# Up projection of a gated MLP: eight half-size block products per feature block become seven, with the operands of tokens and down weights made once

## The chip, the cores and the metric

The kernel runs on one core of one Trainium2 chip. The metric is the device time of one execution in microseconds; the median of three runs counts. The profiled execution is one more run, and its time is given beside its span.

## What is computed

One layer of a streaming encoder over 1024 tokens of width 1024, all in float32: a conditioned normalisation, a combined input projection that feeds four retention heads and a short convolution group, an output projection with a gated residual, and then the part that this change is about, a gated MLP with a causal width-3 convolution over time:

```python
h = modulate(rms_norm(x, norm2_g), sh2, sc2)
u = causal_dwconv(h @ w_up, conv_ffn_w, conv_ffn_b)
ua, ub = jnp.split(u, 2, axis=-1)
x = x + gt2[:, None, :] * ((jax.nn.silu(ua) * ub) @ w_down)
return rms_norm(x, final_g)
```

`w_up` is 1024 x 5632 (the a half and the b half of 2816 columns each), `w_down` is 2816 x 1024, `gt2` is one gate per output column.

## The kernel before

TensorE multiplies a float32 pair as three products of split operands: every operand x is held as hi (x rounded to the fp32r format by a ScalarE cast) and lo (x - hi, a VectorE subtraction), and `mm3` (line 115) issues hi*hi, hi*lo and lo*hi. A matmul takes a stationary 128 x 128 block and 512 moving columns.

The stages follow one another on TensorE, whose instructions keep the order of the program, as `pin` and `mm` say (lines 106 to 113):

1. Front: the first two adaLN vectors from `w_ada`, the transposed normalised tokens, and the v projection. The order of this stage is planned ahead from a table of costs (`run_steps`, line 211). `w_ada` pieces arrive as 512-byte runs (line 277).
2. The k and q projections, retention and the g projection (lines 616 to 786). Between them the other adaLN vectors are summed on VectorE from pieces of `w_ada` (`ada_step`, line 552).
3. Conv stage (line 820): twelve column pieces of `w_in`, 48 matmuls each, with two `ada_step` calls behind each piece.
4. Output projection in three groups of token blocks, (0,1,2), (3,4,5) and (6,7) (`out_mm`, line 879). `norm2` (line 897) makes the residual x1, which stays in SBUF, and its normalised form; `norm2_T` (line 910) transposes a block of 128 tokens, applies scale and shift, and splits the result into the hi and lo of `h2`, the moving operand of the up projection. `h2` is two slabs, one for each half of the tokens.
5. Up stage: for each of 22 feature blocks f, `up` (line 986) loads a 1024 x 128 piece of the a half and one of the b half (512-byte runs, line 729), splits both, and multiplies each with all tokens: 2 pieces x 2 token halves x 8 row blocks x 3 = 96 matmuls. `conv3` (line 815) applies the convolution straight from PSUM, silu and a product follow. After each two feature blocks, `acts_side` and `weights_side` make the operands of the down projection and store them to HBM; GpSimd multiplies the down weights by `gt2` there (line 1029).
6. Down stage: activations and down weights are taken as 2 x 2 blocks, and seven block products of 11 x 12 matmuls (Winograd's form of Strassen's scheme) do the work of eight. `operands` (line 1072) loads one 512 KB tile per step into a ring, casts and subtracts; results are added to x1 from PSUM.
7. Tail (line 1139 on): the last product's results are added, normalised and written.

Instructions on VectorE, ScalarE and the DMA queue of SyncE that are not pinned are ordered when the program is built, by when they are expected to be ready. Tiles come from pools: a tag with `bufs=3` has three buffers, and a tile waits for the release of the one three before it. The raw weight pieces share three buffers (tag `wr`, line 88), their hi and lo forms four each (tags `wh` and `wl`, lines 97 and 98). All DMAs are issued by SyncE.

Of the kernel before, what the change touches and what calls it, by code (L numbers as in the profile page):

```python
# [18 lines left out]
P = 128  # L19
# [51 lines left out]
def layer(ctx: ExitStack, tc: tile.TileContext, a: dict, out: bass.AP):  # L71
# [70 lines left out]
    psum = ctx.enter_context(tc.tile_pool(name="psum", bufs=1, space=PSUM))  # L142
# [24 lines left out]
    stage = slab.tile([P, 4, KT, 256], F32, tag="S2", name="stage")  # L167
# [8 lines left out]
    ada_src = a["w_ada"][:, 0:2048].rearrange("(k p) (s c) -> p k s c", p=P, s=2)  # L176

    def w_in_raw(c0, kp, name):
        raw = raw_tile(name)
        src = a["w_in"][kp * 256 : (kp + 1) * 256, c0 : c0 + 512]  # L180
        nc.sync.dma_start(raw.rearrange("p (k c) b -> p k (c b)", k=2), src.rearrange("(k p) c -> p k c", p=P))
        return raw
# [92 lines left out]
    def ada_src_dma(k, j):  # L275
        w = stage[:, k % 4]
        nc.sync.dma_start(w[:, :, j * P : (j + 1) * P], ada_src[:, :, j, k * P : (k + 1) * P])

    def ada_first(k):
        w = stage[:, k % 4]  # L280
        q_(nc.vector.tensor_scalar(out=w[:, 0], in0=w[:, 0], scalar1=scol[:, 0:1], scalar2=None, op0=ALU.mult))

    def ada_next(k, kt):
        w = stage[:, k % 4]
        q_(mul_add(w[:, 0], w[:, kt], scol[:, kt : kt + 1], w[:, 0]))

    def ada_act(k, kt):
        w = stage[:, k % 4]
        q_(nc.scalar.activation(w[:, kt], w[:, kt], AF.Copy, scale=scol[:, kt : kt + 1]))

    def ada_add(k, i, j):
        w = stage[:, k % 4]
        q_(nc.gpsimd.tensor_tensor(out=w[:, i], in0=w[:, i], in1=w[:, j], op=ALU.add))
# [3 lines left out]
    def ada_mm(k, j, e):  # L297
# [202 lines left out]
    def ada_load(dst, k0, kn, c0, cn):  # L500
        src = a["w_ada"][k0 * P : (k0 + kn) * P, c0 : c0 + cn]
# [29 lines left out]
    def ada_finish(what, hf, c, acc):  # L531
        ps = r1k(f"pada_{what}_{hf}")
        if what[0] == "g":
            dst = (gt1 if what == "g1" else gt2)[:, hf * 512 : (hf + 1) * 512]
            mm(ps, ones, acc)
            nc.vector.tensor_tensor(out=dst, in0=ps, in1=dst, op=ALU.add)
        else:
# [9 lines left out]

    ada = ada_group()
# [21 lines left out]
    cos = cst.tile([P, TB, 64], F32, name="cos")  # L570
    sin = cst.tile([P, TB, 64], F32, name="sin")
# [155 lines left out]
    def w_col_piece(w, c0, name, late=False):  # L727
        raw = raw_tile(name)
        nc.sync.dma_start(raw, w[:, c0 : c0 + P].rearrange("(k p) c -> p k c", p=P))
# [19 lines left out]
    def g_proj(h):  # L749
        w = w_col_piece(a["w_in"], 1536 + h * P, f"wg_{h}")  # L750
# [68 lines left out]

    for f in range(4):  # L820
        pss = []
        for nm, c0 in (("gc", 3072), ("hc", 2048), ("gb", 2560)):
            w = w_col_piece(a["w_in"], c0 + f * P, f"w{nm}_{f}")
            ps = m2k(f"p{nm}_{f}")
            feat_major(w, ps, h1)
            ada_step(2)
            pss.append(ps)
# [48 lines left out]
    x1 = slab.tile([P, TB, D], F32, tag="S0", name="x1")  # L876
    h2 = [slab.tile([P, 2, KT, 512], F32R, tag="S1", name="h2_0"), None]
# [19 lines left out]
    def norm2(ps, tb, add):  # L897
# [6 lines left out]
        add.tensor_tensor(out=x1[:, tb], in0=t, in1=xt, op=ALU.add)  # L904
        ss = sumsq(x1[:, tb], t, f"ss2_{tb}")
        r = rstd_of(ss, D, f"r2_{tb}")
        nc.vector.tensor_scalar(out=t, in0=x1[:, tb], scalar1=r, scalar2=None, op0=ALU.mult)
        xn2[tb] = t

    def norm2_T(tb, on_act=(1, 3, 5, 7), sub=(nc.vector, nc.vector), parts=1):  # L910
        t = xn2[tb]
        s = slice((tb % 4) * P, (tb % 4 + 1) * P)
        hd = h2[tb // 4]
        t3 = t.rearrange("p (k t) -> p k t", k=KT)

        def split_part(i):
            ks = slice(i * KT // parts, (i + 1) * KT // parts)
            hi = hd[:, 0, ks, s]
            nc.scalar.copy(hi, t3[:, ks])
            sub[i].tensor_tensor(out=hd[:, 1, ks, s], in0=t3[:, ks], in1=hi.bitcast(F32), op=ALU.subtract)  # L920

        for q in range(2):
            pt = r1k(f"x1T_{tb}_{q}")
            for k in range(4):
                tr(pt[:, hs(k)], t[:, (4 * q + k) * P : (4 * q + k + 1) * P])
            for i in range(4):
                k = 4 * q + i
                sc, sh = m2[:, k : k + 1], m2[:, 8 + k : 9 + k]
                if k in on_act:
# [295 lines left out]
```

## Time and profile before

| | us |
|---|---|
| median of 3 runs | 1198.0 (1197.68 to 1198.3) |
| the profiled execution | 1197.04 |
| its span in the trace | 1195.2 |
| TensorE busy | 1166.3 |
| VectorE busy | 687.8 |
| ScalarE busy | 394.1 |
| GpSimd busy | 212.8 |

Times of the trace are in microseconds from the start of the span. A row of a group gives the line, the engine, the operation, output and inputs, the shape and the count, then the busy time in all, the mean of one in nanoseconds, and the idle time of the engine just before them with what ended it. TensorE's matmuls overlap, so the duration of one (about 390 ns for 512 columns) is longer than the distance from one to the next.

### The profile page before, as it was taken

How to read it: one execution, taken by the hardware profiler on the slowest of the kernel's cores; microseconds unless marked ns; L12 is line 12 of the kernel's file. 1: busy time of each engine (PE TensorE's matmuls, PEld its weight loads, DVE VectorE, ACT ScalarE, POOL GpSimd, SP SyncE). 2: the span in 40 equal slices, each digit the busy share in tenths (PEclk: the TensorE clock that was granted, in tenths of full speed). 3: DMA queues.
4: the chain of work that ended last, by engine and by line, in shares of the span. 5: the costliest groups of instructions: out<-in, count | busy, mean ns of one | idle time of the engine just before them, and what ended most of it. 6: DMA issues, size and time to landing. Idle time of an engine off the chain costs nothing.

```text
span 1195.2 us, 13885 instructions
## 1 busy us (share of the span) xinstructions
PE 1166.3 (98%) x5356; PEld 967.5 (81%) x5356; DVE 687.8 (58%) x897; ACT 394.1 (33%) x517; POOL 212.8 (18%) x184
## 2 busy tenths in 40 slices
PE   6899999999999999899999999999999999999997
PEld 5788888888888887788888888888888887888885
DVE  6956577555432667656536536545555555665556
ACT  6760123331221445632222222222222224333353
POOL 3503243100000134401110110110110110240023
PEclk9999999999999999999999999999999999999999
DMA  9932423235411264344535525525534449556653
GB/s 297 271 109 68 141 87 91 83 94 169 145 38 56 88 211 146 119 141 159 186 114 177 185 97 176 194 94 171 193 133 162 146 168 362 192 195 193 194 176 124
DMA packets 136110, 183.61 MB, mean 154 GB/s; under 512 B 6996, under 2 KB 85228, under 8 KB 136044
## 3 DMA queue, kind: packets, MB, share of 16 engines
q1 hardware_dynamic: 136044, 182.72, 46.4%
q8 instruction: 42, 0.69, 0.2%
q14 instruction: 24, 0.20, 0.0%
HBM read 138.13 MB, written 44.56 MB: 153 GB/s over the span
## 4 chain that ended last, share of the span: by engine, by line
PE 89%; DVE 4%; issue 2%; POOL 2%; ACT 2%; DMA 1%; SPq 1%; POOLq 0%; DVEq 0%
PE ub L113 20%; PE ua L113 20%; PE po L113 5%; PE pc L113 5%; PE pd L113 5%; PE pa L113 4%; PE pg L113 4%; PE pq L113 4%; PE pk L113 4%; PE pgc L113 4%; PE phc L113 4%; PE pgb L113 4%; PE pb L113 3%; PE pv L113 2%; POOL x L904 1%
## 5 line engine op out<-in xcount | busy, mean ns | idle before, releaser
L113 PE MATMUL ub<-h,wb_h 128*128 128x512 f32 x704 | 218.0, 391 | 0.0
L113 PE MATMUL ua<-h,wa_h 128*128 128x512 f32 x704 | 217.0, 389 | 0.4 <-DVE h L920 0.3
L113 PEld LDWEIGHTS ub<-h,wb_h 128*128 128x128 f32 x704 | 132.9, 189 | 27.5
L113 PEld LDWEIGHTS ua<-h,wa_h 128*128 128x128 f32 x704 | 132.1, 188 | 28.4 <-issue 0.6
L1080 DVE TENSOR_TENSOR op_l<-ring,op_h 128x1024 fp32r<-128x1024 f32 x74 | 96.3, 1307 | 79.9 <-ACT op_h L1079 79.9
L113 PE MATMUL ub<-h,wb_l 128*128 128x512 f32 x352 | 137.7, 391 | 0.0
L113 PE MATMUL ua<-h,wa_l 128*128 128x512 f32 x352 | 136.9, 389 | 0.0
L1029 POOL TENSOR_TENSOR wd<-wd,gt 128x1024 f32<-128x1024 f32 x22 | 53.2, 2442 | 426.1 <-DMA wd<-in_w_down_dram 426.1
L1079 ACT CAST op_h<-ring 128x1024 fp32r<-128x1024 f32 x74 | 78.0, 1054 | 118.6 <-PE pc L113 33.3
L100 DVE TENSOR_TENSOR wb_l<-wb,wb_h 128x1024 fp32r<-128x1024 f32 x22 | 34.4, 1565 | 136.3 <-ACT wb_h L99 136.3
L113 PE MATMUL po<-wo_h,mix 128*128 128x512 f32 x256 | 82.0, 395 | 0.0
L99 ACT CAST wa_h<-wa 128x1024 fp32r<-128x1024 f32 x22 | 23.2, 1054 | 168.5 <-PE ua L113 168.5
L113 PEld LDWEIGHTS ub<-h,wb_l 128*128 128x128 f32 x352 | 66.4, 189 | 13.9
L113 PEld LDWEIGHTS ua<-h,wa_l 128*128 128x128 f32 x352 | 66.1, 188 | 13.8
L100 DVE TENSOR_TENSOR wa_l<-wa,wa_h 128x1024 fp32r<-128x1024 f32 x22 | 28.4, 1290 | 60.8 <-ACT wa_h L99 60.8
L85 DVE SCALAR_TENSOR_TENSOR tb<-ub,fcol,tb 128x1023 f32<-128x1023 f32 (+1 forms) x44 | 56.2, 1278 | 3.0 <-ACT tb L816 2.3
L85 DVE SCALAR_TENSOR_TENSOR act<-ua,fcol,act 128x1023 f32<-128x1023 f32 (+1 forms) x44 | 56.3, 1280 | 0.8
L113 PEld LDWEIGHTS po<-wo_h,mix 128*128 128x128 f32 x256 | 48.1, 188 | 10.4 <-DVE y L836 0.4
L99 ACT CAST wb_h<-wb 128x1024 fp32r<-128x1024 f32 x22 | 23.2, 1054 | 92.2 <-PE ub L113 92.2
L113 PE MATMUL po<-wo_l,mix 128*128 128x512 f32 x128 | 49.9, 390 | 0.0
L99 ACT CAST wo_h<-wo 128x1024 fp32r<-128x1024 f32 x24 | 25.1, 1049 | 62.9 <-PE po L113 20.4
L998 ACT ACTIVATE act<-act 128x1024 f32<-128x1024 f32 x22 | 23.3, 1061 | 61.6 <-DVE act L85 61.6
(264 smaller groups left out, 2370.9 us busy)
## 6 DMA issues: line engine op xcount, KB each, us to landing
ring<-op SPq DMA_DIRECT2D x74, 512.0 KB
wo<-in_w_out_dram SPq DMA_DIRECT2D x24, 512.0 KB
wa<-in_w_up_dram SPq DMA_DIRECT2D x22, 512.0 KB
wb<-in_w_up_dram SPq DMA_DIRECT2D x22, 512.0 KB
op<-sc SPq DMA_DIRECT2D x44, 256.0 KB
wd<-in_w_down_dram SPq DMA_DIRECT2D x22, 512.0 KB
op<-tc SPq DMA_DIRECT2D x44, 256.0 KB
op<-act SPq DMA_DIRECT2D x33, 256.0 KB
```

The source lines that it names most:

```text
L85: return nc.vector.scalar_tensor_tensor(out=o, in0=i0, scalar=s, in1=i1, op0=ALU.mult, op1=ALU.add)
L99: c = nc.scalar.copy(hi, src)
L100: d = nc.vector.tensor_tensor(out=lo, in0=src, in1=hi.bitcast(F32), op=ALU.subtract)
L113: pin(nc.tensor.matmul(ps, st, mv, start=start, stop=stop, skip_group_check=more))
L904: add.tensor_tensor(out=x1[:, tb], in0=t, in1=xt, op=ALU.add)
L998: nc.scalar.activation(ta, ta, AF.Silu)
L1029: nc.gpsimd.tensor_tensor(out=t, in0=t, in1=gt2, op=ALU.mult)
L1079: nc.scalar.copy(hi, raw)
L1080: nc.vector.tensor_tensor(out=lo, in0=raw, in1=hi.bitcast(F32), op=ALU.subtract)
```

## The change

In the up stage the two pieces of one feature block are taken together as a 2 x 2 block matrix (a or b piece; upper or lower half of the 1024 rows), and the tokens as another (upper or lower half of the rows; first or second half of the tokens). Seven products of such blocks, each 4 row blocks x 3 = 12 matmuls, take the place of eight.

- The sums on the tokens' side are made once, in `norm2_T`: two more slabs, `h2[2]` and `h2[3]`, hold them in hi and lo form. For this the transposed blocks of the first four token blocks are also written to HBM (`h_d`) and read back when the block 512 tokens later is there. The lo subtractions that GpSimd made there are now made by VectorE.
- The sums on the weights' side are made per feature block on VectorE (`sum_a`, `sum_b`, `sum_4`), and four weight operands instead of two are split.
- Products that share a partial result share a PSUM bank: ScalarE copies the bank of product 1 into the bank on which products 6, 5 and 3 accumulate (`seed`). Products 1 and 2 of the first three feature blocks run ahead of the others, among the last transposes. `up_slots` writes out the order of TensorE, VectorE and ScalarE for one feature block n: it interleaves the products of n, the convolution, silu and product of n - 1, the operands of the down stage of the pair before, and the sums and splits for n + 1.
- The convolution reads copies in SBUF (`ca`, `cb`) instead of PSUM.
- x1 goes to HBM block by block and is read back ahead of the down stage; the slab it had is that of `h2[2]`.
- The gate `gt2` is no longer multiplied into the down weights. It is stored to HBM and read back, and each result of the down stage is multiplied by it before it is added (`gated_add`, `out_sum`). So the sums of the down weights depend on `w_down` alone; `down_weights` makes them in the conv stage, one of eleven row pairs behind each piece, and stores four of them per pair; the three plain blocks are read from `w_down`.
- In the down stage products 6, 5 and 3 accumulate on a ScalarE copy of product 1's banks and product 4 on product 7's, with all eight banks under one tag; an operand tile is filled by two loads.
- `w_up`, most of `w_in` and the first part of `w_ada` are laid out by the host in the order in which they are loaded, so a partition's part of a piece is one run of 4 KB.

The diff, cut to its core:

```diff
-    stage = slab.tile([P, 4, KT, 256], F32, tag="S2", name="stage")
+    stage = slab.tile([P, 4, 2, KT, P], F32, tag="S2", name="stage")
...
-        nc.sync.dma_start(w[:, :, j * P : (j + 1) * P], ada_src[:, :, j, k * P : (k + 1) * P])
+        nc.sync.dma_start(flat(w[:, j]), a["w_ada1"][k, j])
...
-        nc.sync.dma_start(raw, w[:, c0 : c0 + P].rearrange("(k p) c -> p k c", p=P))
+        nc.sync.dma_start(flat(raw), w[n])
...
+    def down_weights(j):
+        w = [flat(raw_tile(f"wd_{i}_{j}")) for i in range(2)]
+        for i in range(2):
+            f = j + i * NK
+            nc.sync.dma_start(w[i], a["w_down"][f * P : (f + 1) * P, :])
+        t = wts.tile([P, 1024], F32, tag="wh", name=f"tc_{j}", bufs=4)
...
+        tt(t3, b22, b12, ALU.subtract)
+        tt(b12, b12, b11, ALU.subtract)
+        tt(t2, t3, b11, ALU.add)
+        tt(b21, b21, t2, ALU.subtract)
+        for p, src in ((7, t3), (5, b12), (6, t2), (4, b21)):
+            nc.sync.dma_start(w_ops[p, j], src)
...
             feat_major(w, ps, h1)
             ada_step(2)
+            if n_piece[0] < NK:
+                down_weights(n_piece[0])
+            n_piece[0] += 1
...
-        add.tensor_tensor(out=x1[:, tb], in0=t, in1=xt, op=ALU.add)
-        ss = sumsq(x1[:, tb], t, f"ss2_{tb}")
+        add.tensor_tensor(out=xt, in0=t, in1=xt, op=ALU.add)
+        nc.sync.dma_start(x1_d[tb], xt)
+        ss = sumsq(xt, t, f"ss2_{tb}")
...
+        if tb < 4:
+            nc.sync.dma_start(h_d[tb], t)
+            split_h(h2[0], t3, s, KT)
+            return
...
+        tt(c, b22, b12, ALU.subtract)
+        tt(b12, b12, b11, ALU.subtract)
+        split_h(h2[1], t3, s, KT)
+        tt(b11, c, b11, ALU.add)
+        tt(b21, b21, b11, ALU.subtract)
+        split_h(h2[2], u3, s, KT)
...
+    PRODUCTS = {
+        1: ("a", 0, 0, 0, "X", False),
+        2: ("a", 1, 0, 4, "X", True),
+        3: ("4", 0, 1, 4, "Y", True),
+        4: ("b", 1, 2, 4, "Z", True),
+        5: ("b", 0, 1, 0, "Y", True),
+        6: ("s", 1, 2, 0, "Y", True),
+        7: ("s", 0, 3, 0, "Z", False),
+    }
...
+        for k in range(4):
+            c = slice(hf * 512 + k * P, hf * 512 + (k + 1) * P)
+            mm3(S[n][bank], (hi[:, c], lo[:, c]), (b[:, 0, k0 + k], b[:, 1, k0 + k]), k == 0 and not more, k == 3, more)
...
+        if n < N_EARLY:
+            mm(S[n]["Y"], S[n]["a"][0][:, 0:P], h2[0][:, 0, 0])
+        A(S[n]["Y"], S[n]["X"])
...
+    def up_slots(n):
...
+            if not early:
+                up_product(n, 1)
+            lo_of(n, "b")
+        if old:
+            A(S[n - 1]["ca"][:, half[1]], S[n - 1]["Y"])
+            ident_(n - 1, "a")
+        if now:
+            sum_4(n)
+            up_product(n, 7)
+            lo_of(n, "4")
...
+            if not early:
+                seed(n)
+        if old:
+            ident_(n - 1, "b")
+            tap(n - 1, "a", 1)
+        if now:
+            up_product(n, 6)
+            S[n]["p7"] = mlp.tile([P, 512], F32, tag="p7", name=f"p7_{n}")
+            A(S[n]["p7"], S[n]["Z"])
+        if old:
+            tap(n - 1, "a", 2)
+            tap(n - 1, "b", 1)
+        if now:
+            if not early:
+                up_product(n, 2)
+            S[n]["f"] = mlp.tile([P, 512], F32, tag="f", name=f"f_{n}")
+            A(S[n]["f"], S[n]["Y"])
+        if old:
+            ta = S[n - 1]["ta"]
+            pin(nc.scalar.activation(ta, ta, AF.Silu))
+            tap(n - 1, "b", 2)
+            V(ta, ta, S[n - 1]["tb"], ALU.mult)
+        if now:
+            up_product(n, 5)
...
+            hi_of(n + 1, "a", S[n + 1]["wa"])
+            lo_of(n + 1, "a")
+        if now:
+            A(S[n]["ca"][:, half[0]], S[n]["X"])
+        if done is not None:
+            acts_1(done)
+        if now:
+            up_product(n, 4)
+            V(S[n]["cb"][:, half[1]], S[n]["Y"], S[n]["p7"], ALU.add)
+        if done is not None:
+            acts_2(done)
+        if new:
+            sum_a(n + 1)
+        if now:
+            up_product(n, 3)
+        if new:
+            sum_b(n + 1)
+        if now:
+            V(S[n]["cb"][:, half[0]], S[n]["Z"], S[n]["f"], ALU.add)
+        if new:
+            lo_of(n + 1, "s")
...
+    up_product(0, 1)
+    seed(0)
+    up_product(0, 2)
+    norm2_T(6, bank_t)
+    up_product(1, 1)
+    seed(1)
+    up_product(1, 2)
+    norm2_T(7, bank_t)
+    up_product(2, 1)
+    seed(2)
+    up_product(2, 2)
...
+    x1 = slab.tile([P, TB, D], F32, tag="S0", name="x1")
+    for tb in range(TB):
+        nc.sync.dma_start(x1[:, tb], x1_d[tb])
...
-        nc.sync.dma_start(raw, ops[p, j])
+        nc.sync.dma_start(raw[:, half[0]], a_ops[p, j])
+        if p in W_AT:
...
+            nc.sync.dma_start(raw[:, half[1]], a["w_down"][f * P : (f + 1) * P, half[c]])
+        else:
+            nc.sync.dma_start(raw[:, half[1]], w_ops[p, j])
...
     def out_sum(tb):
-        pin(add_to(tb, 1, pa[tb]))
+        t = f_[tb]
+        pin(nc.vector.tensor_tensor(out=t, in0=pa[tb], in1=gt2[:, half[1]], op=ALU.mult))
+        o = x1[:, tb, half[1]]
+        pin(nc.vector.tensor_tensor(out=o, in0=t, in1=o, op=ALU.add))
```

`sum_a`, `sum_b` and `sum_4` are five VectorE operations on 128 x 512 elements per feature block, `acts_1` and `acts_2` four per two blocks with seven stores of 256 KB, `ident_` and `tap` the three steps of the convolution, `hi_of` and `lo_of` the cast and the subtraction of one operand.

More of the change, by code (lines that the diff above doesn't have):

```diff
@@ L140, in rows @@
         nc.sync.dma_start(dst, src.rearrange("(r q) -> r q", q=P))
[L142 removed]
+    psum_pool = tc.tile_pool(name="psum", bufs=1, space=PSUM)
+    psum = psum_pool.__enter__()
+    dram = ctx.enter_context(tc.tile_pool(name="dram", bufs=1, space=bass.MemoryType.DRAM))
+    NK = NF // 2
+    half = [slice(0, 512), slice(512, 1024)]
     def m2k(name):
@@ L536, in ada_finish @@
             nc.vector.tensor_tensor(out=dst, in0=ps, in1=dst, op=ALU.add)
+            if what == "g2" and hf == 1:
+                nc.sync.dma_start(gt2_d, gt2)
         else:
@@ L958, in layer @@
     mix_pool.__exit__(None, None, None)
[L961 to L971 removed]
+    mlp_pool = tc.tile_pool(name="mlp_pool", bufs=1)
@@ new lines, in layer, with keep, acts_1 @@
+    a_ops = {(p, j): dram.tile([P, 512], F32, name=f"aop_{p}_{j}") for p in range(1, 8) for j in range(NK)}
+    def keep(p, j, src):
+        nc.sync.dma_start(a_ops[p, j], src)
+    def acts_1(j):
+        a1, a2 = S[2 * j]["ta"], S[2 * j + 1]["ta"]
+        a11, a21, a12, a22 = a1[:, half[0]], a1[:, half[1]], a2[:, half[0]], a2[:, half[1]]
+        keep(1, j, a11)
+        keep(2, j, a12)
+        keep(4, j, a22)
+        s1 = mlp.tile([P, 512], F32, tag="c1", name=f"s1_{j}")
+        V(s1, a21, a22, ALU.add)
+        keep(5, j, s1)
+        V(a21, a11, a21, ALU.subtract)
+        keep(7, j, a21)
@@ L1046, in layer @@
+    up_product(0, 1)
[9 more added lines that the diff above has]
+    up_product(2, 2)
+    for tb in range(4, 8):
+        t3_split(tb)
+    load_a(0)
+    load_b(0)
+    sum_a(0)
+    sum_b(0)
+    lo_of(0, "s")
+    for n in range(NP + 1):
+        up_slots(n)
     fg = cst.tile([P, D], F32, tag="row", name="fg", bufs=2)
     nc.sync.dma_start(fg, a["final_g"].partition_broadcast(P))
-    acts = {}
@@ L1049, in layer @@
-    wa, wb = up_mm(0)
-    first = m2k("ua_0"), m2k("ub_0")
-    feat_major(wa, first[0], h2_of, (0,))
-    ub0 = feat_units(wb, first[1], h2_of, (0,))
-    fill(ub0, 1)
-    norm2_T(6, sub=(nc.gpsimd,))
-    fill(ub0, 4)
-    norm2_T(7, parts=2)
-    fill(ub0, 9)
-    second = up_mm(fseq[1])
-    feat_major(wa, first[0], h2_of, (1,))
-    feat_major(wb, first[1], h2_of, (1,))
-    for j in range(NK):
-        for i in range(2):
-            f = j + i * NK
-            acts[f] = up(f, first if f == 0 else None)
-        acts_side(j, acts[j], acts[j + NK])
-        weights_side(j)
+    gt2 = cst.tile([P, D], F32, tag="row", name="gt2_again", bufs=2)
@@ L1092, in product, with banks, four, gated_add @@
                 step_mm(ps, op, j, i, start)
-    def banks_m(name):
-        t = [m2k(f"{name}_{i}") for i in range(2)]
+    def banks(name):
+        return [psum3.tile([P, 512], F32, tag="d", name=f"{name}_{i}", bufs=8) for i in range(4)]
+    def four(name):
+        t = [dp.tile([P, 1024], F32, tag=name, name=f"{name}_{i}", bufs=2) for i in range(2)]
         return [t[i // 2][:, half[i % 2]] for i in range(4)]
-    def banks_r(name):
-        return [r1k(f"{name}_{i}") for i in range(4)]
-    def add_to(tb, side, src, eng=nc.vector):
+    def gated_add(tb, side, src):
+        t = w4(f"gt_{tb}_{side}")[:, half[0]]
+        nc.vector.tensor_tensor(out=t, in0=src, in1=gt2[:, half[side]], op=ALU.mult)
         o = x1[:, tb, half[side]]
-        return eng.tensor_tensor(out=o, in0=src, in1=o, op=ALU.add)
+        return nc.vector.tensor_tensor(out=o, in0=t, in1=o, op=ALU.add)
     def square_half(tb, c, junk, name):
```

313 lines of the change are left out of this document (186 added, 127 removed).

## The prediction

> **What bounds the kernel now.** I read the page first, for the share of the chain by engine; then the chain of waits in order of time, for TensorE's pace and the joints between stages; then windows cut at those joints; then the groups of VectorE and ScalarE, which must carry the new work.
>
> ```profile
> span 1195.2 us, 13885 instructions
> ...
> PE 89%; DVE 4%; issue 2%; POOL 2%; ACT 2%; DMA 1%; SPq 1%; POOLq 0%; DVEq 0%
> ```
>
> TensorE holds 89% of the chain that ended last. The profiled execution took 1197.04 us, 1.84 us more than its span and 0.96 us less than the median of 1198.0; I count against 1197.04 and add the 0.96 at the end. This kernel's runs agree so well that 0.2% (2.4 us) tells a change.
>
> ```profile
> 299.81 10.88 PE phc L113 x48
> ...
> 497.74 1.09 PE x1T L121 x8
> ...
> 517.92 10.88 PE ua L113 x48
> ...
> 964.00 10.67 PE ub L113 x47
> ...
> 989.46 1.15 DVE op_l L1080
> 990.65 16.39 PE pa L113 x71
> ...
> 1178.09 8.93 PE pd L113 x38
> ```
>
> A matmul follows the one before it after 10.88 / 48 = 0.2267 us. From 517.92 to 974.7 the up stage is one unbroken row of such pieces; at its two ends stand joints with VectorE work in them. The windows show the same, and what the other engines have to spare (columns: length, then busy time of PE, PEld, DVE, ACT, POOL with counts, clock, DMA share, GB/s):
>
> ```profile
> 0.00:57.40 57.40, 43.59 (x203) 37.59 (x203) 44.20 (x82) 39.59 (x76) 25.04 (x40) 0.94 0.98 296
> 254.40:319.70 65.30, 65.30 (x302) 54.40 (x301) 33.81 (x43) 12.62 (x13) 0.00 (x0) 1.00 0.39 119
> 459.40:488.30 28.90, 26.67 (x128) 21.47 (x127) 21.63 (x27) 15.74 (x25) 15.85 (x11) 1.00 0.55 175
> 488.30:517.90 29.60, 27.06 (x119) 21.68 (x118) 17.00 (x22) 16.06 (x28) 11.62 (x8) 0.94 0.34 106
> 517.90:974.70 456.80, 456.80 (x2017) 378.24 (x2016) 239.95 (x228) 113.24 (x107) 47.50 (x20) 1.00 0.45 153
> 974.70:990.70 16.00, 14.05 (x63) 11.31 (x61) 14.89 (x14) 7.42 (x7) 5.75 (x2) 1.00 0.78 294
> ```
>
> In the up stage TensorE never rests while VectorE works 53% of the time and the DMA queue carries 45%: fewer matmuls there shorten the kernel until another engine fills its slot.
>
> **The matmuls.** The loops fix their number: 22 feature blocks x 7 products x 12 = 1848 for 22 x 96 = 2112, so 264 x 0.2267 = 59.8 us less, if each slot of 84 (19.04 us) stays full. Three dummy matmuls add 0.7. Each still has one weight load and 512 moving columns, so the pace has no reason to change.
>
> **Does VectorE fit into 19.04 us?** Its groups inside the old up stage:
>
> ```profile
> L85 DVE SCALAR_TENSOR_TENSOR act<-ua,fcol,act 128x1023 f32<-128x1023 f32 (+1 forms) x42 | 53.7, 1279 | 0.7
> ...
> L100 DVE TENSOR_TENSOR wb_l<-wb,wb_h 128x1024 fp32r<-128x1024 f32 x20 | 32.0, 1599 | 134.8 <-ACT wb_h L99 134.8
> L1001 DVE TENSOR_TENSOR act<-act,tb 128x1024 f32<-128x1024 f32 x21 | 25.7, 1225 | 0.7
> L100 DVE TENSOR_TENSOR wa_l<-wa,wa_h 128x1024 fp32r<-128x1024 f32 x19 | 23.3, 1224 | 57.6 <-ACT wa_h L99 57.6
> L1005 DVE TENSOR_TENSOR sc<-act,sc 128x512 f32<-128x512 f32 x20 | 13.7, 684 | 0.0
> ```
>
> ```profile
> L1029 POOL TENSOR_TENSOR wd<-wd,gt 128x1024 f32<-128x1024 f32 x22 | 53.2, 2442 | 426.1 <-DMA wd<-in_w_down_dram 426.1
> ```
>
> The same subtraction costs 1224 ns for wa_l and 1599 for wb_l, beside which GpSimd's L1029 runs; that multiplication leaves the stage, so I take 1224. Per feature block: three long splits 3.67, four taps 5.12 (PSUM source before, SBUF now; same price), one product 1.23, and seven half-length operations (sum_4, its split, three sums, two cb additions) at 684: 4.79. Together 14.8 us; every second slot has the four sums of acts as well, 17.5. A pair takes 32.3 of 38.08 us.
>
> ScalarE, with the PSUM copy priced by the down stage's:
>
> ```profile
> L816 ACT ACTIVATE act<-ua,fcol 128x1024 f32<-128x1024 f32 x21 | 25.3, 1206 | 0.0
> ...
> L998 ACT ACTIVATE act<-act 128x1024 f32<-128x1024 f32 x22 | 23.3, 1061 | 61.6 <-DVE act L85 61.6
> ...
> L99 ACT CAST wa_h<-wa 128x1024 fp32r<-128x1024 f32 x19 | 20.0, 1055 | 165.3 <-PE ua L113 165.3
> ```
>
> ```profile
> L1115 ACT COPY p<-pa 128x512 f32<-128x512 f32 x4 | 2.2, 586 | 0.1
> ```
>
> Three long casts and silu 4.2, two identities 2.4, six half copies or casts 3.5: 10.1 of 19.04. No row shows a copy from PSUM to PSUM (the seed); I price it at 0.59.
>
> Totals are not enough, since all three engines are pinned. In a full slot the tightest hand-over is cb's first half: product 5 ends at 13.6, product 3 overwrites the bank from 16.3 on. Ahead of the addition VectorE has one long split, two half operations, four taps, the product, the split for n + 1 and two sums: 11.5 us, plus 1.2 for a cast and for silu that it waits for, so with a start 0.7 into the slot it is free at 13.4 and done at 14.3. The split of s then ends at 19.6 and is wanted by product 7 of the next slot at 21.8. Both have 2 us to spare, so a full slot costs nothing extra. DMA: 1 MB of weights and 0.9 MB of stores per 19 us is 102 GB/s, less than the 153 of now. The first three slots have only 60 matmuls, 13.6 us, and the third holds 17.5 of VectorE: 3.9 us late (0 to 5).
>
> **The entry into the up stage.** Product 7 of block 0 needs h2[3], made last, on VectorE. What VectorE does there now:
>
> ```profile
> L100 DVE TENSOR_TENSOR wo_l<-wo,wo_h 128x1024 fp32r<-128x1024 f32 x21 | 27.6, 1324 | 8.1 <-ACT wo_h L99 8.1
> L932 DVE TENSOR_SCALAR t<-x1T,m 128x128 f32<-128x128 f32 x28 | 10.5, 406 | 5.2 <-PE x1T L121 4.8 <-ACT t L930 0.2
> L907 DVE TENSOR_SCALAR t<-x,r 128x1024 f32<-128x1024 f32 x8 | 10.3, 1285 | 7.7 <-POOL r L157 7.7
> L903 DVE TENSOR_TENSOR t<-po,gt 128x512 f32<-128x512 f32 x16 | 9.9, 682 | 0.0
> ...
> L904 DVE TENSOR_TENSOR x<-t,xr 128x1024 f32<-128x1024 f32 x1 | 2.6, 2645 | 2.9 <-DMA xr<-in_x_dram 2.9
> ```
>
> From 459.4 on, where group (3,4,5) ends, VectorE now has: ten L903 6.8, five L907 6.4, one L904 2.6, six wo_l still to come 7.9, block 3's scales and split 2.8, blocks 4 to 7 with four half sums and two splits each 20.7, three wa_l 3.7, the h2[3] splits 2.7, the first sums and s split 3.3. That is 56.9 us, so 516.3; TensorE's 171 matmuls and 40 transposes of 0.136 are 44.3 us, so 503.7. VectorE decides, and I take 517. The low end is 512 (L907 and L904 without the GpSimd beside them that their length hints at); the high end 521, if VectorE is filled to the 92% of the densest stretch below. From there 1776 matmuls, 402.6 us, and the 3.9 above: the stage ends at 923.5, not 974.7: **-51.2**. This contains the 59.8, less 8.6 for the entry.
>
> **Front.**
>
> ```profile
> 20.00:40.00 20.00, 17.78 (x85) 15.51 (x84) 18.45 (x35) 15.24 (x31) 9.14 (x13) 0.83 1.08 287
> 1000.00:1020.00 20.00, 20.00 (x90) 16.56 (x89) 10.82 (x10) 10.50 (x13) 0.00 (x0) 1.00 0.88 337
> ```
>
> The queue is full to 57.4 us and moves 296 / 0.98 = 302 GB/s with many 512-byte runs; the down stage's 4 KB rows move 337 / 0.88 = 383. But VectorE is busy 18.45 of 20 in the thick of it, so at most 8% of the stretch, 4.4 us, can go. I take **-1.5** (0 to -4.4), nearer to VectorE's row. The Trainium skill, page "DMA: Bandwidth & Descriptors", section Specifications, puts the least transfer for line rate at 512 bytes; by it this term is 0 and the result 1151.5. The trace does not agree, as far as two different stages can be compared: 302 against 383 GB/s.
>
> **Conv stage.** Added per piece of 10.88 us: two loads of 512 KB, four stores of 256 KB (2.1 MB, 193 GB/s) and four half operations on VectorE, 2.7 us, where it has half its time free. With the 119 GB/s of now the queue must carry 312 in the first five pieces, between 81% and 103% of the two rates above. The tighter thing is the three raw buffers, and SyncE's queue, in which the stores wait for the sums with the next piece's load behind them.
>
> ```profile
> 269.06 0.37 SPq L729 DMA_DIRECT2D whc<-in_w_in_dram  x1
> ```
>
> ```profile
> 274.12 1.05 ACT L99 CAST whc_h<-whc 128x1024 fp32r<-128x1024 f32 x1 [7.73 <-DMA whc<-in_w_in_dram]
> ```
>
> A load takes 5.1 us. With that, a weight piece holds its buffer 7.4 us, an ada piece 6.6 (two operations), a down piece 12.9 (load, sums, store at a load's price): 46.4 / 3 = 15.5 us per piece while ada pieces still come (five), 33.2 / 3 = 11.1 after. Short by 5 x 4.6 + 6 x 0.2 = 24 us. Against it stands the lead: this whc is multiplied at 299.81, 24 us after its cast. The low end is 0 (lead kept, or runs of 4 KB quicker), the high end 24 (lead gone, as the sums also take one of four hi buffers). I take **+4**, nearer to the lead's row.
>
> **Into the down stage and out of it.** TensorE rests 1.95 of the 16 us from 974.7. Now fg, gt2 and x1 (5.2 MB) must be loaded there too.
>
> ```profile
> 969.47 1.75 SPq L1076 DMA_DIRECT2D ring<-op  x4
> ...
> 985.27 0.80 SPq L971 DMA_DIRECT2D op<-act  x2
> ```
>
> The queue already puts ring loads ahead of the last block's stores, by readiness; the ring's slab is free 8 us before the stage ends, x1's 2.7 before. So the operands should come first: **0** (-1.4, the rest being one PSUM copy, to +14, 5.2 MB at 337 GB/s less the 2 of now). The bank copies in front of products 6 and 4 (0.59) end while the other three banks are worked on: nothing. One more VectorE step stands in the tail:
>
> ```profile
> 1187.03 0.70 DVE x L1103
> ```
>
> **+0.7.** Sum: -51.2 - 1.5 + 4 + 0 + 0.7 = -48.0; 1197.04 - 48.0 = 1149.0, with the 0.96 **1150**.
>
> **The rivals.**
>
> *Clean joints* (0.13): no conv wait, entry at 512, third slot on time: 4 + 5 + 3.9 less, 1137. For it: ScalarE and DMA have room. Against: VectorE's 56.9 us.
>
> *Conv stage starved* (0.17): the whole 24, so 1170. For it: 15.5 us against 10.88. Against: the lead. It shows as TensorE waiting for VectorE's weight splits between 254 and 390.
>
> *x1 ahead of the operands* (0.05): +14, 1164.
>
> *Hand-overs each slot* (0.05), the slower side. TensorE waits wherever its fixed order meets VectorE's or ScalarE's, as it did at the transposes:
>
> ```profile
> PE x1T L121 <- DVE t L907: 2.4, 2, 2.1
> PE x1T L121 <- ACT t L930: 2.0, 2, 1.7
> ```
>
> Two such waits per slot, in front of products 5 and 3, would be 2.1 + 1.7 = 3.8 us, times 22 = 84: 1234. It is slower than before from (1198 - 1150) / 22 = 2.2 us per slot on. For it: the clock, which falls to 0.83 in the front where TensorE waits often. Against: the 2 us of slack. The Trainium skill, page "TensorE: Matmul & The Clock Gate", section "A second HAM failure mode: psum-queue depth-cycling", says that a kernel cycling through PSUM banks can idle so often between groups of matmuls that the clock keeps dropping. The trace of before cannot show that for groups of 12; its groups of 48 keep 1.00.
>
> That the matmuls would not become fewer can't be; the loops count them.
>
> **How the numbers follow.** The forecast has 0.60, the rivals the 0.40 above. The range takes in the three faster rivals and the bounds of the entry: 1135 to 1171; what it leaves out is the slower rival and sums of several mishaps. All cases but one are faster by far more than 0.2%: faster 0.94, same 0.01, slower 0.05.
>
> **What would show it.** Up pieces of x12 in the chain with no gaps from the fourth block on, 19.04 us per block; the first product 7 near 517; VectorE near 80% there; a short wait for weight splits in the conv stage; ring loads ahead of x1's. I am wrong if the up stage's TensorE share falls below 95%, or if the time goes at a joint by more than the ends given.

## The result and the profile after

The changed kernel takes 1185.7 us (median of 4 runs, 1182.0 to 1188.7), the kernel before 1197.8 beside it: a ratio of 0.990 (95% interval 0.987 to 0.993). It is faster, but by a quarter of what was forecast. In the profiled executions the span falls from 1195.2 to 1184.2, by 11.0 us where 48.0 were worked out: 37 us are missing.

The page of the changed kernel first: span, busy time by engine, and the shares of the chain that ended last.

```profile
span 1184.2 us, 13766 instructions
...
PE 1118.7 (94%) x5095; PEld 922.0 (78%) x5095; DVE 819.0 (69%) x1104; ACT 504.6 (43%) x698; POOL 129.2 (11%) x146
...
PE 68%; DVE 12%; DMA 10%; ACT 3%; POOL 3%; issue 3%; SPq 1%; POOLq 0%; DVEq 0%; ACTq 0%
```

TensorE's part of the chain has fallen from 89% to 68%; VectorE and the DMA queue hold 22% of it. Cut at TensorE's own instructions (starts of the first or last matmul of a kind in the timelines of both kernels), the difference comes from these pieces:

| from ... to ... | before | after | difference | forecast |
|---|---|---|---|---|
| start, first matmul of k | 82.25 | 80.98 | -1.3 | -1.5 |
| last matmul of the conv stage | 306.97 | 314.05 | +7.1 | +4 |
| last of the output projection | 99.90 | 99.74 | -0.2 | 0 |
| last of the up stage | 485.37 | 458.31 | -27.1 | -51.2 |
| last matmul of all | 212.12 | 220.86 | +8.7 | 0 |
| end of the span | 8.59 | 10.26 | +1.7 | +0.7 |

The up stage itself came out as forecast. The windows of the changed kernel from the first product 7 to the last up matmul, and of the 60 us around its beginning (columns as before):

```profile
500.00:520.00 20.00, 10.62 (x43) 8.43 (x44) 12.68 (x14) 7.28 (x14) 4.47 (x5) 0.70 0.48 170
520.00:540.00 20.00, 10.69 (x38) 8.05 (x36) 9.75 (x13) 8.34 (x16) 0.00 (x0) 0.81 0.00 1
540.00:560.00 20.00, 17.47 (x67) 13.96 (x68) 10.62 (x15) 7.66 (x10) 0.00 (x0) 0.84 0.16 52
...
546.90:953.50 406.60, 403.79 (x1776) 332.67 (x1775) 325.55 (x359) 206.54 (x255) 0.00 (x0) 1.00 0.31 107
```

1776 matmuls in 406.6 us, 2.8 us of waits in 22 slots, VectorE at 80%. But this stretch begins at 546.9 and not at 517. From 500 to 540 TensorE works half the time at a granted clock of 0.70 to 0.81, and VectorE, which was to be the bound there, works only 12.68 and 9.75 of 20 us. The chain of waits shows what goes on (start, length, piece):

```profile
507.97 0.61 DVE t L933
508.58 0.14 issue
508.72 4.56 PE X L113 x12
...
525.06 1.04 ACT h L947
526.10 0.49 ACT Y L1018
526.64 5.49 PE X L113 x12
532.13 0.73 PE x1T L121 x4
532.88 2.91 ACT t L966 x8
535.82 0.70 DVE t L827
...
540.27 1.04 ACT h L947
541.31 0.49 ACT Y L1018
541.85 5.04 PE X L113 x12
546.89 2.72 PE Z L113 x12
```

TensorE's waits between 490 and 550 (total, times, longest) and two rows of VectorE's timeline with the idle time before them:

```profile
PE X L113 <- DVE t L933: 13.6, 1, 13.6
PE X L113 <- ACT Y L1018: 11.8, 3, 5.6
```

```profile
520.61 0.69 DVE L827 TENSOR_TENSOR t<-t 128x512 f32<-128x512 f32 x1 [6.89 <-ACT t L966]
...
535.82 0.69 DVE L827 TENSOR_TENSOR t<-t 128x512 f32<-128x512 f32 x1 [8.46 <-ACT t L966]
```

The output projection's last matmul starts at 494.77. The first early product needs PSUM banks that come free when VectorE has multiplied the last result by the gate (L933), and those four multiplications stand in VectorE's queue among sums and splits of older blocks: 13.6 us. (One of these splits, at 501.45, takes 3.31 us instead of 1.22 beside an addition on GpSimd, which is 2.1 of the 13.6.) Then product 2 of block 1 waits for its seed (Y, L1018), which stands on ScalarE behind the cast of token block 6 (h, L947); that cast waits for VectorE's sums, these for the transposes, and TensorE issues the transposes of block 7 only behind that product 2. So each of these two token blocks is a loop through three engines, 15 us long (517.0 to 531.9), in which every one of them rests. After such a wait 12 matmuls take 5.49 us instead of 2.72. In sum from the last matmul of the output projection: 25.4 us of waits, 72 matmuls, 3 dummies and 16 transposes for 19.2 at their usual pace, and 7.4 that remain, by which the matmuls behind the waits are slower while the granted clock is low: 52.0 in all where the forecast had 27.9.

### The profile page after: what moved, and what is told of

Its sections match the earlier page's. It is cut to its first block, busy times and chain, and to the rows that moved or that the text cites. A ratio compares the mean times of both kernels' runs of the same rounds, so it can differ in the third digit from the quotient of the medians.

```text
span 1184.2 us, 13766 instructions
## 1 busy us (share of the span) xinstructions
PE 1118.7 (94%) x5095; PEld 922.0 (78%) x5095; DVE 819.0 (69%) x1104; ACT 504.6 (43%) x698; POOL 129.2 (11%) x146
## 4 chain that ended last, share of the span: by engine, by line
PE 68%; DVE 12%; DMA 10%; ACT 3%; POOL 3%; issue 3%; SPq 1%; POOLq 0%; DVEq 0%; ACTq 0%
PE Y L113 15%; PE X L113 10%; PE Z L113 10%; PE pb L113 5%; PE pc L113 5%; PE pa L113 4%; PE pq L113 4%; PE pk L113 4%; PE pv L113 2%; DMA wd<-in_w_down_dram 2%; PE po L113 2%; PE pg L113 2%; POOL xr L934 1%; DMA ada_g<-in_w_ada_dram 1%; DMA ada_sh<-in_w_ada_dram 1%
## 5 line engine op out<-in xcount | busy, mean ns | idle before, releaser
L1275 DVE TENSOR_TENSOR op_l<-ring,op_h 128x1024 fp32r<-128x1024 f32 x74 | 90.1, 1224 | 83.6 <-ACT op_h L1274 81.7
L113 PE MATMUL X<-h,a_h 128*128 128x512 f32 x352 | 113.6, 405 | 25.4 <-DVE t L933 13.6
L113 PEld LDWEIGHTS X<-h,a_h 128*128 128x128 f32 x352 | 68.5, 196 | 41.3 <-issue 14.0
L113 PE MATMUL X<-h,a_l 128*128 128x512 f32 x176 | 70.7, 401 | 0.0
L1018 ACT CAST s_h<-st 128x1024 fp32r<-128x1024 f32 x22 | 23.2, 1053 | 102.7 <-DVE st L1015 102.7
L85 DVE SCALAR_TENSOR_TENSOR act<-ca,fcol,act 128x1023 f32<-128x1023 f32 (+1 forms) x44 | 56.4, 1281 | 1.3 <-ACT act L1116 0.5
L85 DVE SCALAR_TENSOR_TENSOR tb<-cb,fcol,tb 128x1023 f32<-128x1023 f32 (+1 forms) x44 | 56.3, 1280 | 0.7
L113 PE MATMUL Y<-h,b_h 128*128 128x512 f32 x176 | 54.5, 391 | 2.0 <-ACT f L1018 2.0
L113 PE MATMUL Z<-h,s_h 128*128 128x512 f32 x176 | 54.2, 389 | 0.0
L113 PE MATMUL Y<-h,s_h 128*128 128x512 f32 x176 | 54.2, 389 | 0.0
L113 PE MATMUL Z<-h,b_h 128*128 128x512 f32 x176 | 54.2, 389 | 0.0
L113 PE MATMUL pb<-op_l,op_h 128*128 128x512 f32 x132 | 51.6, 391 | 2.6 <-DVE op_l L1275 2.6
```

Source lines behind the costliest of these rows:

```text
L85: return nc.vector.scalar_tensor_tensor(out=o, in0=i0, scalar=s, in1=i1, op0=ALU.mult, op1=ALU.add)
L113: pin(nc.tensor.matmul(ps, st, mv, start=start, stop=stop, skip_group_check=more))
L1018: return pin(nc.scalar.copy(o, i))
L1275: nc.vector.tensor_tensor(out=lo, in0=raw, in1=hi.bitcast(F32), op=ALU.subtract)
```

## The experiments

Theory 1: the entry is a chain of hand-overs, and it, the conv stage, the way into the down stage and the tail lose their time independently of each other. The rival for the entry is the prediction's own step: VectorE's total work sets it. "Entry" below is the time from the last matmul of the output projection to the first product 7: 52.0 us in the changed kernel. All edits are to the changed kernel.

**The order of the early products.**

```diff
     up_product(0, 1)
     seed(0)
-    up_product(0, 2)
     norm2_T(6, bank_t)
     up_product(1, 1)
     seed(1)
-    up_product(1, 2)
     norm2_T(7, bank_t)
     up_product(2, 1)
     seed(2)
-    up_product(2, 2)
+    for n in range(3):
+        up_product(n, 2)
```

> Edit: the early products are reordered. Products 1 of blocks 0, 1 and 2 come first, with the transposes of token block 6 behind the first and those of block 7 behind the second; the three products 2 follow. Nothing is taken from any engine. Theory 1 (the entry is a chain of hand-overs): in the changed kernel product 2 of blocks 1 and 2 wait 5.6 us each for the seed, which stands behind a cast on ScalarE, and the transposes of block 7 come 14.9 us after those of block 6. Here the transposes of 7 come about 6 us after those of 6, no product 2 waits for a seed, and the first product 7 starts at 533 to 538 us instead of 546.9: 9 to 14 us less, about 1174 us in all. Rival (the prediction's step): VectorE's total work sets the entry; it is unchanged, so product 7 stays at 546 to 548 and the time at 1186.

1173.2 us, ratio 0.978 (0.976 to 0.980); entry 40.0 us, 12.0 less, first product 7 at 533.7. TensorE's waits there:

```profile
PE X L113 <- DVE t L933: 13.6, 1, 13.6
PE X L113 <- ACT Y L1018: 2.9, 1, 2.9
```

The 11.8 us for seeds have become 2.9 (none was expected), the 13.6 for the banks stand as they were. No engine has less to do, so the rival falls: the order alone was worth 12 us.

**VectorE's work, added.**

```diff
     seed(0)
+    scr = mlp.tile([P, 512], F32, tag="scr", name="scr")
+    for _ in range(8):
+        V(scr, S[0]["Y"], h2[0][:, 0, 0].bitcast(F32), ALU.add)
     up_product(0, 2)
```

> Edit: eight additions of 128x512 on VectorE (8 x 0.68 = 5.4 us) whose result nobody uses are put behind the first seed, into the 6.9 us that VectorE idles before the sums of token block 6. The output stays the reference's. Theory 1: they are hidden, the first product 7 stays at 546 to 548. Rival (VectorE's total work sets the entry): product 7 comes 5.4 us later, at 552.

1187.6 us; entry 52.2 us, and TensorE's waits are the same to a tenth (13.7 and 11.8). 5.4 us more on VectorE cost 0.2, which is nothing: in the five other profiles that have the changed kernel's entry it takes 50.3 to 52.6.

**The banks.**

```diff
+    t67 = {tb: w4(f"t1_{tb}") for tb in (6, 7)}
+    for tb in (6, 7):
+        for ch in range(2):
+            A(t67[tb][:, ch * 512 : (ch + 1) * 512], ps[tb][ch])
     for n in range(2):
         load_a(n)
```

(`norm2` then multiplies t67 by the gate, and the squares that it sums for blocks 6 and 7 keep the order of the program on ScalarE.)

> Edit: the four PSUM banks of token blocks 6 and 7 are copied to SBUF by ScalarE as soon as the output projection ends, and VectorE multiplies by the gate from there; so the old PSUM pool comes free without VectorE. VectorE's work is the same, ScalarE has 4 x 0.59 = 2.4 us more. Theory 1: the first early product, which started at 508.72 after 13.56 us of waiting for VectorE's multiplication, starts at 499 to 502; the transposes of block 6 come 6 to 8 us earlier, the loop of 15 us per block behind them stays, and the first product 7 is at 538 to 541 instead of 546.9: 1178 to 1180 us in all. Rival (VectorE's total work): product 7 stays at 546 to 548, 1186.

1180.5 us, ratio 0.984 (0.983 to 0.985); entry 47.4. Counted from the end of the output projection, the first early product starts after 5.2 us instead of 14.0, as expected; the transposes of block 6 come 6.2 us sooner, the loop behind them stays, and 4.5 us of the gain arrive. The rival falls here too. What was late next is the load of x for block 6: SyncE issues it at 497.0, behind five loads of up weights, where the changed kernel issues it at 487.8, behind two.

**Both.**

> Edit: the two edits before together. Theory 1: the gains add up until VectorE's work, without idle time between 494 and the end of its splits, is the bound: first product 7 at 525 to 530, 1166 to 1170 us in all. Rival A: the low clock of this stretch (0.70 to 0.84, 4.6 to 5.5 us for 12 matmuls where 2.7 is usual) stays, and TensorE alone needs 72 matmuls at half speed and the waits: 533 or later. Rival B (VectorE's total work from the beginning): 546 to 548.

1172.4 us, ratio 0.977 (0.975 to 0.979); entry 39.0. The number is rival A's, but the reason is another one: with the reordering done the banks bring only 1 us, because TensorE now waits 6.1 us for the normalised block 6, whose load of x is late as in e_early_banks. Neither expectation had that.

**Both, mended** (against e_early_both).

```diff
+    x67 = {6: x_again(6)}
     t67 = {tb: w4(f"t1_{tb}") for tb in (6, 7)}
+    x67[7] = x_again(7)
...
     up_product(0, 1)
     seed(0)
-    norm2_T(6, bank_t)
     up_product(1, 1)
     seed(1)
+    norm2_T(6, bank_t)
+    up_product(2, 1)
+    seed(2)
     norm2_T(7, bank_t)
-    up_product(2, 1)
-    seed(2)
```

> Edit: as e_early_both, with two things mended: x is loaded for token blocks 6 and 7 into buffers that are free before the output projection ends (in e_early_both that load was issued at 496.7, after its end, and set the transposes of block 6, at 509.7), and the products 1 of blocks 0 and 1 both run ahead of the transposes of 6. Theory 1: the transposes of block 6 come at 507 to 509, those of block 7 at 512 to 515, no product 2 waits, and the first product 7 starts at 525 to 529 (533 in e_early_both): 1163 to 1168 in all. Rival (from about 533 on VectorE's own work is the bound, as the prediction had it): product 7 stays at 532 to 534, with VectorE without gaps from 494 on.

1173.4 us, ratio 0.978 (0.975 to 0.981). The entry is 34.2 us, 4.8 less than in e_early_both, but the time is the same: this run's conv stage took 2.3 us more, and from the first product 7 to the end of the up stage it takes 409.3 instead of 406.3. These 3 us are lost in that product 7 itself: it starts after a wait of 4.1 us and takes 5.64 instead of 2.72, with 0.6 of waiting for its split and slower matmuls (granted clock 0.82 from 532.1 to 545.7). From its end to the end of the stage it is 403.6 in the changed kernel and here. Counted to the end of that product, the entry has gained 1.9 on e_early_both. No product 2 waits for its seed any more. What waits now is product 7, for the cast of its weight sums on ScalarE, which starts as soon as VectorE has made them, and VectorE is busy 30.18 of the 34.21 us:

```profile
PE Z L113 <- ACT s_h L1024: 4.1, 1, 4.1
```

```profile
497.92:532.13 34.21, 21.86 (x93) 16.75 (x91) 30.18 (x36) 25.94 (x46) 5.37 (x5) 0.87 0.34 118
```

So the prediction's bound may hold here after all, below the chain of hand-overs. The test is e_early_dve's edit once more, on this kernel:

> Edit: the eight unused additions of e_early_dve (5.4 us on VectorE) put into e_early_3. From the last matmul of the output projection to the first product 7 the changed kernel takes 52.0 us, e_early_3 34.2; in the changed kernel the additions cost nothing. If, with the hand-overs gone, VectorE's amount of work is the bound (it rests about 3 us of the 41 from 493 on in e_early_3), the first product 7 comes 2.5 to 5.5 us later, at 36.7 to 39.7 us. If the chain of hand-overs from the transposes of block 7 on is still the bound, it stays at 34 to 35.5.

1179.7 us; entry 38.2, 4.0 more (its conv stage, which the edit does not touch, took 3.5 more as well). TensorE's wait for the same cast:

```profile
PE Z L113 <- ACT s_h L1024: 6.1, 1, 6.1
```

The same additions cost 0.2 us in the changed kernel and 4.0 of their 5.4 here, in one run each: with these hand-overs gone, VectorE's work is most of the bound.

**The conv stage.**

```diff
+        d = wts.tile([P, 1024], F32, tag="wl", name=f"td_{j}", bufs=4)
+        t5, t4 = d[:, half[0]], d[:, half[1]]
-        tt(b12, b12, b11, ALU.subtract)
+        tt(t5, b12, b11, ALU.subtract)
...
-        tt(b21, b21, t2, ALU.subtract)
+        tt(t4, b21, t2, ALU.subtract)
...
```

> Edit: the sums of the down weights are all written to tiles of their own (two of them to a buffer of the kind of the lo operands), so the two raw buffers of a pair come free with the sums, not with the stores, about 4 us earlier. Same bytes, same operations. From the end of the v projection to the end of the conv stage the kernel before takes 307.3 us and the changed one 314.4. Theory 1 (three raw buffers are too few): 308 to 311, that is 3 to 6 us less, about 1181. Rival (the DMA queue at 245 to 274 GB/s is itself the bound): 313 to 315, no change; with one more of four lo buffers taken it can also lose.

1179.3 us, ratio 0.984 (0.982 to 0.985). From the first to the last matmul the stage took 135.0 us before and 142.4 after the change; here it takes 135.0 again. The changed kernel's waits between 250 and 396, which have all gone here, and the windows of the stage, first the changed kernel's, then this one's:

```profile
PE pgb L113 <- ACT wgb_h L99: 1.9, 1, 1.9
PE phc L113 <- ACT whc_h L99: 1.8, 1, 1.8
PE pgb L113 <- DVE wgb_l L100: 0.5, 1, 0.5
PE phc L113 <- DVE whc_l L100: 0.5, 1, 0.5
```

```profile
252.60:395.40 142.80, 138.03 (x606) 112.51 (x605) 81.37 (x101) 27.78 (x28) 4.78 (x2) 0.99 0.74 252
```

```profile
254.90:390.00 135.10, 135.10 (x605) 111.48 (x604) 80.83 (x100) 27.64 (x27) 4.88 (x2) 1.00 0.77 262
```

The same bytes go through at 262 GB/s instead of 252, so the queue's rate was not the bound; the raw buffers, held until the stores had landed, were.

> Edit: only the first of the eleven row pairs of the down weights is loaded, summed and stored in the conv stage; the down stage takes its four sums from that pair for all steps, so the result is not the reference's. Both theories expect the conv stage to end 307 to 308 us after the v projection, as in the kernel before: 7 us less, about 1179. If more than 2 us of the loss stay, it is not the down weights that cost it, but the way in which the pieces of w_in are loaded.

1176.2 us, with ten of the eleven row pairs left out; the stage takes 135.0 us too. All of the loss was that of the down weights' step.

**Into the down stage.** SyncE's queue in the changed kernel after the last up matmul (start, time in the queue, instruction):

```profile
950.78 3.71 SPq L1257 DMA_DIRECT2D x<-x_d  x8
955.34 0.32 SPq L1265 DMA_DIRECT2D ring<-aop  x1
958.16 0.33 SPq L1269 DMA_DIRECT2D ring<-in_w_down_dram  x1
964.59 0.80 SPq L1127 DMA_DIRECT2D aop<-act  x2
...
969.69 0.32 SPq L1246 DMA_DIRECT2D gt_again<-gt_d  x1
970.05 0.42 SPq L1265 DMA_DIRECT2D ring<-aop  x1
```

x1's eight loads stand ahead of the last five operands of product 1; behind them and one more operand come the last stores, which wait until 964.6 for the activations, then fg and gt2, whose two buffers those stores release. The next operand is issued at 970.05, and TensorE waits 2.9 us for its cast.

```diff
-    for tb in range(TB):
-        nc.sync.dma_start(x1[:, tb], x1_d[tb])
     n_raw = [0]
...
     product(1, pa, True)
+    for tb in range(TB):
+        nc.sync.dma_start(x1[:, tb], x1_d[tb])
```

> Edit: the eight loads that bring x1 back stand behind the operand loads of product 1 in the program, so that SyncE issues all eleven operands of product 1 ahead of them. In the changed kernel the first product of the down stage ends 38.1 us after the last matmul of the up stage, where its eleven steps take 29.9. Theory 1 (x1 ahead of the operands, and with it the stores that SyncE waits for): at most 32 us between the two, 6 us less in all, about 1180. Rival (what holds the operands are the two buffers of fg and gt2, which wait for the last stores): the wait stays, 1186; a second rival is that the x1 loads now collide with the operands of product 6: the time comes back there, 1186, with product 1 quick and product 6 late.

1181.8 us, ratio 0.986 (0.984 to 0.988). Product 1 ends 31.9 us after the up stage instead of 38.3; of these 6.4 us, 1.0 is lost again in the products behind. All eleven operands now stand ahead of x1 in the queue:

```profile
956.84 0.43 SPq L1267 DMA_DIRECT2D ring<-in_w_down_dram  x1
957.49 2.28 SPq L1308 DMA_DIRECT2D x<-x_d  x4
965.39 0.80 SPq L1127 DMA_DIRECT2D aop<-act  x2
```

The two buffers alone:

```diff
-    fg = cst.tile([P, D], F32, tag="row", name="fg", bufs=2)
...
-    gt2 = cst.tile([P, D], F32, tag="row", name="gt2_again", bufs=2)
...
+    late = slab.tile([P, 2, D], F32, tag="S2", name="late")
+    fg, gt2 = late[:, 0], late[:, 1]
...
```

> Edit: fg and gt2 are loaded into the slab that h2[1] leaves, not into the two buffers of the last activations. x1 stays ahead of the operands. If the buffers of fg and gt2 hold the operands up: product 1 ends 32 us after the up stage instead of 38.1, about 1180 in all. If x1 and the last stores ahead of the operands in SyncE's queue do (theory 1): 36 to 40 us, 1184 to 1188.

1188.2 us; 40.4 us from the up stage to the end of product 1. So it is the place in the queue behind x1 and the last stores, not the buffers of fg and gt2.

**The first GpSimd operation of the final stage.** GpSimd's and VectorE's timelines of the changed kernel:

```profile
1146.13 6.08 POOL L160 TENSOR_SCALAR r<-ss 128x1 f32<-128x1 f32 x1 [633.20 <-ACT y_out L166]
1152.29 0.55 POOL L161 TENSOR_TENSOR r<-r,nhalf 128x1 f32<-128x1 f32 x1
```

```profile
1146.33 0.69 DVE L1298 TENSOR_TENSOR gt<-f,gt_again 128x512 f32<-128x512 f32 x1
1146.93 1.22 DVE L1275 TENSOR_TENSOR op_l<-ring,op_h 128x1024 fp32r<-128x1024 f32 x1
1148.07 0.69 DVE L1300 TENSOR_TENSOR x<-gt,x 128x512 f32<-128x512 f32 x1
1148.67 3.49 DVE L1275 TENSOR_TENSOR op_l<-ring,op_h 128x1024 fp32r<-128x1024 f32 x3
1152.88 1.28 DVE L1338 SCALAR_TENSOR_TENSOR y_out<-x,r,fg 128x1024 f32<-128x1024 f32 x1 [0.72 <-POOL r L161]
```

One value per partition, 6.08 us, ending when VectorE's row of six operations ends (1152.16). The four final outputs wait 2.3 us in all for GpSimd's results (0.72 the first), splits stand behind those outputs, and TensorE waits 2.6 us for two of these splits.

```diff
+    warm = cst.tile([P, 1], F32, name="warm")
+    nc.gpsimd.tensor_scalar(out=warm, in0=p7[3][:, 0:1], scalar1=1.0 / D, scalar2=EPS, op0=ALU.mult, op1=ALU.add)
     product(4, pa, False)
```

> Edit: one small GpSimd operation (128x1) is put ahead of product 4, some 40 us before the final stage, with nobody waiting for its result. In the changed kernel the first GpSimd operation after 633 us takes 6.08 us where the others take 0.2 to 1.3. Theory C (GpSimd is slow at first after a long rest): the added operation takes about 6 us and the one of the final stage at most 1.3, and TensorE's wait of 2.6 us for a split behind it goes: 1183. Theory L (it is held while VectorE runs its row of additions and splits without a gap, from 1146.3 to 1152.2): the added operation is short, as VectorE rests 1.5 us in each step there, and the one of the final stage still takes 6.08: 1186.

1185.2 us. Both operations are long:

```profile
1114.75 6.91 POOL L1329 TENSOR_SCALAR warm<-p 128x1 f32<-128x1 f32 x1 [602.14 <-DVE p L1326]
1145.09 6.08 POOL L160 TENSOR_SCALAR r<-ss 128x1 f32<-128x1 f32 x1 [23.43 <-ACT y_out L166]
```

```profile
1115.78 1.29 DVE L1300 TENSOR_TENSOR x<-gt,x 128x512 f32<-128x512 f32 x2
1116.98 4.63 DVE L1275 TENSOR_TENSOR op_l<-ring,op_h 128x1024 fp32r<-128x1024 f32 x4
```

The second kept its 6.08 after a rest of 23 us, so theory C falls. Theory L's detail was wrong too (VectorE did not rest there), but its reason agrees with the rows: the added operation ends at 1121.66, VectorE's row at 1121.61.

**All together.** e_early_3, e_conv_bufs and e_x1_late, and in the last product:

```diff
-    tail = {j: operands(3, j) for j in range(KB, NK)}
+    tail = {j: operands(3, j, pin) for j in range(KB, NK)}
```

(`operands` passes its cast and split through `pin`, and so does `final` its output.)

> Edit: e_early_3, e_conv_bufs and e_x1_late together, and in the last product the splits of its last four steps pinned ahead of the final outputs on VectorE. Theory 1 (the loss against the prediction lay in joints that are independent of each other): 18 to 21 us less by the entry, 7 by the conv stage, 4 to 6 by the way into the down stage, 1 to 2 by the tail: 30 to 36 less than the 1185.7 of the changed kernel, 1150 to 1156. Rival (the joints feed each other: an earlier conv stage or up stage meets loads that are not there yet): less than 25, above 1160.

1164.4 us, ratio 0.971 (0.969 to 0.973): 21 less than the changed kernel, a number of the rival's. Its reason, loads that are not there yet, does not show: the entry takes 34.2, the conv stage 135.0, product 1 ends 32.2 after the up stage, so the three joints keep 17.8, 7.4 and 6.1 us side by side. Lost again are 2.9 in the first product 7, as in e_early_3, and 4.8 at the end: the last matmul comes 1.5 us earlier behind product 1, but the span ends 16.6 us after it instead of 10.3. So without the pins:

> Edit: e_all without the pinned splits of the last product. In e_all the last matmul comes 180.99 us after the first of the second down product, where the changed kernel takes 182.52, but the span ends 16.6 us behind it instead of 10.3: VectorE had the four final outputs in one piece in front of the last sums. Theory 1 (VectorE, not TensorE, sets the end of the tail, so the pinned splits cost 16.6 + 181.0 - 10.3 - 183.5 = 3.8 us against e_x1_late): the two pieces are 183.5 and 10.3 again, 1160 to 1161 in all. Rival (the loss in e_all is from the joints that meet, and the tail only shows it): 1163 to 1165 as e_all.

1161.4 us, ratio 0.970 (0.967 to 0.972), the lowest median here. Its interval overlaps that of e_all, and the front, which no edit touches, is 2.5 us shorter in its profile, so the pins are judged by the pieces. From the start of the second down product to the last matmul 185.2, then 10.2 to the end: 195.4 instead of e_all's 197.6. The pins cost 2.3, not 3.8; they moved TensorE's wait (0.8 us for splits in e_all, 3.3 here) to VectorE, which was late at the end.

## Why the prediction was wrong, point by point

- **The matmuls, the slots, the hand-overs in each slot: right.** 406.6 us from the first product 7 on, where 402.6 and 3.9 were worked out; the waits in all 22 slots are 2.8 us and the clock is 1.00, so the slower rival did not come true. Nor did, in these slots, the rule of the Trainium skill that stood beside it (page "TensorE: Matmul & The Clock Gate", section "A second HAM failure mode: psum-queue depth-cycling").
- **The entry: the step that failed.** "VectorE decides, and I take 517": 56.9 us of VectorE's work against 44.3 of TensorE's. It was 546.9; 24.1 of the missing 37 us are here. The larger of two sums is a lower bound, and it was taken for the forecast, with a high end that only filled VectorE less densely. What bound it was the order: banks that were freed from the middle of VectorE's queue, and seeds behind a cast. e_early_order, e_early_banks and e_early_dve show that; The sum itself was good: from 29.7 us before the end of the output projection, where the prediction begins to count, VectorE is busy 55.7 us up to the first product 7 in the changed kernel, but these take 81.7, as it rests 26. e_early_3 and e_early_3_dve show VectorE's bound, which lies below: 34 us after the output projection, 27.9 in the forecast. There VectorE is busy 52.7 of 63.9 us counted in the same way; it rests 7.2 before the output projection ends and 4.0 after it, where the forecast had no rest at all. For the full slots the prediction said "Totals are not enough" and went through the hand-overs; at the entry it did not.
- **Conv stage: mechanism right, term mis-sized.** +7.1 instead of +4, by the three raw buffers, as e_conv_bufs shows.
- **Into the down stage: wrong.** "So the operands should come first": six of eleven did. 6.4 us instead of 0, by the mechanism of the third rival (x1 ahead of the operands), at half its price.
- **Tail: mis-sized.** 1.7 after the last matmul instead of 0.7, and 2.6 ahead of it, behind GpSimd's small operations, which the prediction did not look at. The first is VectorE's: in the chain the last sums follow one another at 3.2 us, where TensorE takes 2.72 for a block:

```profile
1172.72 0.60 DVE f L1362
...
1175.94 0.60 DVE f L1362
```

- **Front: undecided.** -1.3 against -1.5, but in the kernels here, which all have the changed front, k begins between 80.3 and 83.2, against 82.25 before. These profiles cannot tell a gain from none, nor the prediction's term from the 0 that it worked out from the Trainium skill, page "DMA: Bandwidth & Descriptors", section Specifications.

With three joints mended 1161.4 is reached, inside the range that was given; the rest to 1150 is mostly the entry (35.1 instead of 27.9) and an up stage of 409.7 instead of 406.5 behind it. The second is all in the first product 7, which takes 6.1 us instead of 2.72 behind its wait; from its end on the stage takes 403.6 us, as in the changed kernel.

## What to carry to other kernels

At a joint between two stages, the sum of each engine's work is a floor. Write down the order on every engine and follow one item through (which queue frees the bank, what stands ahead of the seed, what the DMA queue is waiting for when it reaches the load that is needed); the joint costs the longest chain of these, and reordering may return it without removing any work. A source buffer that is also the store's source is held for the store's time: give results their own tile if the next load wants the buffer.

## What the runs showed of the hardware

A GpSimd operation that reads one value per partition was held for a whole row of VectorE operations with two inputs in SBUF: 6.08 us in the changed kernel, 6.91 in e_pool_warm, ending within 0.1 us of the row's last one. The next one of the same kind in the changed kernel takes 1.29 beside a single VectorE output of 1.28. The other way round, in e_early_3 VectorE's split waits for GpSimd's addition and takes 3.39 us instead of 1.22:

```profile
503.36 3.39 DVE L827 TENSOR_TENSOR a_l<-wa,a_h 128x1024 fp32r<-128x1024 f32 x1
```

```profile
502.92 2.75 POOL L938 TENSOR_TENSOR xr<-t,xr 128x1024 f32<-128x1024 f32 x1 [18.69 <-DVE t L937]
```

The Trainium skill, page "SBUF — State Buffer", section "SBUF: two separate sides", says that the two share a pair of ports which the one that starts first keeps for its whole instruction, if VectorE's has two inputs in SBUF and GpSimd's reads SBUF. The second pair of rows agrees: the addition ends at 505.67, and with the split's own 1.22 that makes 506.89, where it ends at 506.75. The first goes further: if the ports are what held it, GpSimd did not get them between two VectorE instructions that follow each other without a gap. The prediction gave such an operation no price; in these two dense VectorE stretches it lasted as long as what was left of the stretch.

After a wait, 12 matmuls took 4.6 to 5.5 us instead of 2.72, with a granted clock of 0.70 to 0.84 in these windows; so the waits of the entry came with slower matmuls behind them. How much of the entry the clock alone cost was not tried apart from the waits.

The conv stage is not the same in each execution: in the ten profiles that have the changed kernel's, it takes 140.6 to 147.8 us, in the four where it was mended, or left out but for a first pair, 135.0. Four executions of the changed kernel lie between 1182.0 and 1188.7 us; whether the conv stage makes this difference was not tested, and the kernel before, too, lay between 1195.3 and 1203.7 in the nine executions beside e_all_2.
